# A gated feed-forward block: 19 of 22 gate-and-up pairs as seven quadrant products

## The chip, the cores and the metric

The kernel runs on one core of one Trainium2 chip, in one launch. The metric is device time in microseconds (us). Engines: TensorE (PE) multiplies, with PSUM banks as its output; VectorE (DVE), ScalarE (ACT) and GpSimd (POOL) do the elementwise work; SyncE (SP) and POOL issue DMAs. Each engine runs its own instructions strictly in program order and waits on semaphores for the others.

## The reference, cut to what matters

Two layers over 512 tokens of width 1024, each with a token mixer, a cross-attention and a gated feed-forward block. The change lies in the last one:

```python
D_MODEL = 1024; SEQ = 512; DEPTH = 2
D_FF = 2816                      # worked out: 22 blocks of 128 features

def swiglu_ffn(u, w_gate_up, w_down):
    g, up = jnp.split(u @ w_gate_up, 2, axis=-1)
    return (jax.nn.silu(g) * up) @ w_down

for i in range(DEPTH):
    ...                          # mixer, cross-attention
    u = rms_norm(h, ffn_pre_g[i])
    y = swiglu_ffn(u, w_gate_up[i], w_down[i])
    h = h + rms_norm(y, ffn_post_g[i])
```

## The kernel before

All matrices are float32. PE takes them in a rounded form (float32r), so each operand is split into a high part, a rounded copy, and a low part, the rest. A product is then three matmuls: high by high, low by high, high by low. A split is one ACT copy and one subtraction, mostly on DVE, for weights (L238, L239, in `issue`) as for activations (L201, L202, in `split`).

The normed activations u of a layer stand transposed in `uh` and `ul`: 128 partitions, 8 blocks k of 128 input features, 512 tokens. `norm_block` makes them a block of 128 tokens at a time: a square sum on ACT (L266), mean and power on POOL (L273, L278), scaling on DVE (L299), PE transposes (L285), and the split of these (L289, L290).

A weight tile is 128x1024, 512 KB: 8 blocks k for 128 output features. `plan` is the list of all weight tiles in the order of use. `fetch` loads them on SP's queue (L222) into one of two staging buffers `raw0` and `raw1`, and `issue` splits them into a ring of three pairs `wh`, `wl`. `used` gives a ring buffer back. A later tile is loaded as soon as the subtraction has left its staging buffer.

`ffn_up` makes gate and up for 22 pairs of feature blocks: 44 weight tiles, gate and up by turns, in `feats`. The output is features by tokens, 128x512, one PSUM bank. For each tile there are 8 blocks k times three matmuls of 512 columns (L313, L314, L315). The first three tiles run in two halves of 256 tokens, since the second half of u isn't normed yet; the norm's last transposes come between these matmuls. The silu of gate is an ACT instruction (L1065), its product with up a DVE one (L1069), and the split of that product (L201, L202) follows at once, into the tiles `r0` to `r21`.

`close` is the down product: 11 chunks of weights, each with two blocks k of 128 features, four token blocks and 24 matmuls of 512 columns (L365 to L367). Its first weights are loaded and split while `ffn_up` still runs. The gates of its spare weight buffers are in `ffn_spares`.

Instructions are written in this order by generators that `drive` runs. A scheduler then sets each engine's order from its own estimates; PE's order stays as written only where `pin` says so, which is not the case in the steady part of `ffn_up`.

Of the kernel before, what the change touches and what calls it, by code (L numbers as in the profile page):

```python
# [7 lines left out]
F32 = mybir.dt.float32  # L8
F32R = mybir.dt.float32r
# [9 lines left out]
NB = S // P  # L19
DK = D // P  # L20
FT = 22
NMEM = 256
EPS = 1e-6
NEG = -1e30
# [17 lines left out]
class Null:  # L42
# [3 lines left out]
    def __call__(self, *a, **k):  # L46
        return Null()


class Trunk:  # L50
    def __init__(self, tc, t, stack):
        self.tc = tc
        self.t = t
        pool = stack.enter_context(tc.tile_pool(name="sb", bufs=1))
        psum = stack.enter_context(
            tc.tile_pool(name="ps", bufs=1, space=bass.MemoryType.PSUM)
        )

        def sb(name, shape, dt=F32):
            return pool.tile(shape, dt, name=name)  # L60

        self.h = [sb(f"h{b}", [P, D]) for b in range(NB)]
# [12 lines left out]
        self.rc = sb("rc", [P, S])  # L75
        self.rs = sb("rs", [P, S])
        self.small = sb("small", [P, 160])
        self.qz = [sb(f"qz{i}", [P, 2, S], F32R) for i in range(2)]
        self.half = sb("mhalf", [P, 1])
        self.lam = sb("lam", [P, 1])  # L80
        self.gsub = sb("gsub", [P, 1])
        self.bank = [psum.tile([P, S], F32, name=f"bank{i}") for i in range(8)]

    def run(self):
        self.plan = []
        self.nc, self.planning = Null(), True
        self.emit()
        self.nc, self.planning = self.tc.nc, False
        self.emit()

    def reset(self):
# [10 lines left out]
        self.sbanks = self.bank[4:6]  # L102


    def pick(self, what, items):
# [102 lines left out]

    def plain(self, i):

        return None if self.planning else self.pool.tile([P, D], F32, name=f"m{i}", tag=f"r{i}")

    def restore(self, i):
        if not self.planning:
# [2 lines left out]
    def staging(self, i):  # L217
        return self.extra[i - 2] if i in (2, 3, 4) else self.raw[i % 2]

    def fetch(self, upto):  # L220
        while not self.planning and self.loaded < min(upto, len(self.plan)):
            self.nc.sync.dma_start(self.staging(self.loaded), self.plan[self.loaded][0])  # L222
            self.loaded += 1

    def issue(self):
        while not self.planning and self.issued < len(self.plan):
# [11 lines left out]
            self.nc.scalar.activation(hi, raw, AF.Copy)  # L238
            (self.nc.gpsimd if eng else self.nc.vector).tensor_tensor(  # L239
                lo, raw, hi.bitcast(F32), ALU.subtract  # L240
            )
# [105 lines left out]
            evac(bank)  # L347


    def close(self, w, ktiles, act, ready, gpost, gnext, spares, between=None):  # L350

        nc = self.nc
        yg = self.f[0:4]
# [93 lines left out]
    def setup(self):  # L447
# [3 lines left out]

        self.extra = [self.plain(i) for i in (4, 5, 6)]
        nc.vector.memset(self.half, -0.5)
        for z in self.qz:
            nc.gpsimd.memset(z[64:128, 0].bitcast(F32), 0.0)
            nc.gpsimd.memset(z[0:64, 1].bitcast(F32), 0.0)
        x(0)
        g = None
        for w in self.FIRST:
# [360 lines left out]
    def mixer(self, kind, wqk, wv, memory):  # L820
        hd = 64 if kind == 0 else 128
        if kind == 1:
            self.ones = self.mask[:, 0:P]
            self.nc.vector.memset(self.ones, 1.0 / P)

# [224 lines left out]
    XORDER = "k2 q1 k3 q2 q3"  # L1050


    def a_slot(self, k):
        return self.R[16 + k] if k < 6 else self.R[2 + k] if k < 14 else self.R[k - 14]

    def ffn_up(self, w):
        nc = self.nc
        keep = {}

        def evac(i):  # L1060
# [12 lines left out]
            return fn  # L1073

        yield from self.feats([(w[i], evac(i)) for i in range(2 * FT)], 3)

    def emit(self):
        self.reset()
# [3 lines left out]
            return self.R[k][:, 0], self.R[k][:, 1]  # L1082

        def a_act(k):
            return self.a_slot(k)[:, 0], self.a_slot(k)[:, 1]

        def o_ready(k):
            return ("o", k) in self.mark
# [13 lines left out]
        def has(*key):  # L1102
# [15 lines left out]
        ]  # L1118
        ffn_spares = [
            (None, None),  # L1120
            ((8, 9), has("n1", 3)),
            ((16, 17), has("n1", 0)),
            ((18, 19), has("n1", 1)),
            ((20, 21), has("n1", 2)),
        ]

        self.setup()
# [2 lines left out]
        for i in range(2):  # L1130
# [38 lines left out]
            self.drive(dense, self.x_attention(), self.RATE[2])  # L1169
            for k in range(11):  # L1170
                self.mark.pop(("n1", k), None)
            if i == 0:
# [4 lines left out]
            self.drive(  # L1177
                chain(
                    self.ffn_up(t["gate_up"][i]),
                    self.close(  # L1180
                        t["down"][i], FT, a_act, None, get("ffn_post_g"),
                        get("mix_pre_g") if i == 0 else None, ffn_spares,
                    ),
                )
            )
# [26 lines left out]

def alternate(a, b):
    return np.stack([a, b], 1).reshape((2 * a.shape[0],) + a.shape[1:])


def constants():
# [14 lines left out]
def layout(i):  # L1232
# [8 lines left out]
    for n in "ab":  # L1241
# [11 lines left out]
    r["gate_up"] = np.stack(  # L1253
        [alternate(feature_tiles(w[:, :ff]), feature_tiles(w[:, ff:])) for w in i["w_gate_up"]]
    )
# [25 lines left out]
```

## Time and profile before

| what | value |
|---|---|
| median of 3 runs | 1648.62 us (1646.05 to 1649.39) |
| profiled execution | 1650.47 us, its span 1648.7 us |
| PE busy | 1607.1 us, 97% |
| DVE, ACT, POOL busy | 54%, 42%, 17% |
| HBM read | 148.51 MB |

The profile is one execution. In its rows "L313" is line 313 of the kernel; buffer numbers are left out of names; "idle before <-" is the time in which the engine stood still before this group and what released it. In the timeline a row is start, length, engine, line, operation, output and inputs, shape and count. Matmuls overlap, so the time of one is the distance between starts. The gate-and-up stages are at about 473 to 715 us and 1281 to 1522 us.

### The profile page before, as it was taken

The numbers are of one execution on the slowest core, as the hardware profiler recorded it, in microseconds if no ns is written. First come the engines' busy times: TensorE is split into PE (matmuls) and PEld (weight loads), VectorE is DVE, ScalarE is ACT, GpSimd is POOL, SyncE is SP. The second block draws the span as 40 slices with busy tenths as digits, with TensorE's granted clock in tenths as the row PEclk, the third lists the DMA queues.
The fourth block names the chain that finished last, engine by engine and source line by source line (L and its number), as shares of the span: only waits on it lengthen the run. The fifth ranks groups of instructions, "written<-read, shape, count | busy, mean of one in ns | idle before, by whom it ended". The sixth has DMA issues, their size and how long they took to land.

```text
span 1648.7 us, 22174 instructions
## 1 busy us (share of the span) xinstructions
PE 1607.1 (97%) x8696; PEld 1384.9 (84%) x8696; DVE 896.1 (54%) x1414; ACT 696.9 (42%) x1211; POOL 276.3 (17%) x268
## 2 busy tenths in 40 slices
PE   6999989999999999999999999989999999999998
PEld 6899878899888888888798888778987988888886
DVE  7778886745553333322367888856555433333233
ACT  4566665544443232222336565634444322323121
POOL 4634420200010000000044654320001000000000
PEclk9999999999999999999999999999999999999999
DMA  5533423333312323222424434333331232232322
GB/s 217 150 89 103 112 76 107 116 115 100 118 64 94 102 90 103 95 98 99 131 87 134 123 98 115 100 105 104 115 115 65 77 103 92 100 101 92 103 89 89
DMA packets 54856, 172.49 MB, mean 105 GB/s; under 512 B 7520, under 2 KB 7776, under 8 KB 54752
## 3 DMA queue, kind: packets, MB, share of 16 engines
q1 hardware_dynamic: 54752, 171.08, 32.6%
q8 instruction: 68, 1.11, 0.3%
q14 instruction: 36, 0.29, 0.1%
HBM read 148.51 MB, written 2.10 MB: 91 GB/s over the span
## 4 chain that ended last, share of the span: by engine, by line
PE 81%; DVE 8%; DMA 3%; POOL 3%; issue 3%; ACT 2%; SPq 0%; POOLq 0%; DVEq 0%; ACTq 0%
PE bank L314 14%; PE bank L313 14%; PE bank L315 14%; PE bank L365 7%; PE bank L367 7%; PE bank L366 7%; PE bank L285 4%; PE bank L725 2%; PE bank L651 1%; PE bank L652 1%; DVE wl L239 1%; PE bank L634 1%; PE bank L635 1%; PE bank L920 1%; PE bank L633 1%
## 5 line engine op out<-in xcount | busy, mean ns | idle before, releaser
L238 ACT ACTIVATE wh<-raw 128x1024 fp32r<-128x1024 f32 x231 | 244.6, 1059 | 551.7 <-PE bank L314 224.2
L239 DVE TENSOR_TENSOR wl<-raw,wh 128x1024 fp32r<-128x1024 f32 x204 | 257.1, 1260 | 354.5 <-ACT wh L238 353.7
L313 PE MATMUL bank<-uh,wh 128*128 128x512 f32 (+1 forms) x1184 | 443.2, 375 | 0.4 <-ACT uh L289 0.4
L314 PE MATMUL bank<-ul,wh 128*128 128x512 f32 (+1 forms) x1184 | 442.7, 374 | 0.0
L315 PE MATMUL bank<-uh,wl 128*128 128x512 f32 (+1 forms) x1184 | 442.6, 374 | 0.0
L313 PEld LDWEIGHTS bank<-uh,wh 128*128 128x128 f32 x1184 | 223.7, 189 | 39.5 <-ACT uh L289 0.8
L315 PEld LDWEIGHTS bank<-uh,wl 128*128 128x128 f32 x1184 | 223.8, 189 | 38.2 <-issue 0.5
L314 PEld LDWEIGHTS bank<-ul,wh 128*128 128x128 f32 x1184 | 223.8, 189 | 38.0 <-DVE ul L290 0.3
L273 POOL TENSOR_SCALAR small<-small 128x1 f32<-128x1 f32 x76 | 24.2, 318 | 1105.3 <-ACT junk L266 1105.1
L365 PE MATMUL bank<-wh,r 128*128 128x512 f32 x400 | 157.9, 396 | 1.2 <-DVE f L761 0.8
L366 PE MATMUL bank<-wl,r 128*128 128x512 f32 x400 | 156.8, 392 | 0.0
L367 PE MATMUL bank<-wh,r 128*128 128x512 f32 x400 | 155.0, 392 | 0.0
L285 PE MATMUL bank<-ident,f 128*128 128x128 f32 x576 | 95.8, 282 | 22.8 <-DVE f L299 17.4
L1069 DVE TENSOR_TENSOR f<-f,bank 128x512 f32<-128x512 f32 x44 | 30.3, 688 | 142.6 <-PE bank L315 141.1
L285 PEld LDWEIGHTS bank<-ident,f 128*128 128x128 f32 x576 | 71.3, 144 | 33.5 <-DVE f L299 20.1
L365 PEld LDWEIGHTS bank<-wh,r 128*128 128x128 f32 x400 | 75.6, 189 | 18.5 <-DVE f L761 1.6
L366 PEld LDWEIGHTS bank<-wl,r 128*128 128x128 f32 x400 | 75.7, 189 | 15.0 <-issue 0.2
L367 PEld LDWEIGHTS bank<-wh,r 128*128 128x128 f32 x400 | 75.3, 189 | 15.4
L365 PE MATMUL bank<-r,r 128*128 128x512 f32 x208 | 83.7, 403 | 0.0
L366 PE MATMUL bank<-r,r 128*128 128x512 f32 x208 | 81.9, 394 | 0.4 <-DVE r L239 0.4
L367 PE MATMUL bank<-r,r 128*128 128x512 f32 x208 | 80.1, 395 | 0.0
L289 ACT ACTIVATE r<-bank 128x512 fp32r<-128x512 f32 x104 | 60.7, 592 | 38.2 <-PE bank L285 33.1
(173 smaller groups left out, 2764.7 us busy)
## 6 DMA issues: line engine op xcount, KB each, us to landing
raw<-in_gate_up SPq DMA_DIRECT2D x88, 512.0 KB, 3.2
raw<-in_down SPq DMA_DIRECT2D x44, 512.0 KB, 3.2
r<-r SPq DMA_DIRECT2D x120, 128.0 KB, 2.3
raw<-in_x_wk SPq DMA_DIRECT2D x16, 512.0 KB, 3.3
raw<-in_x_wv SPq DMA_DIRECT2D x16, 512.0 KB, 3.3
raw<-in_x_wq SPq DMA_DIRECT2D x16, 512.0 KB, 3.3
raw<-in_x_wo SPq DMA_DIRECT2D x16, 512.0 KB, 3.3
raw<-in_b_qk SPq DMA_DIRECT2D x16, 512.0 KB, 3.4
```

The source lines that it names most:

```text
L238: self.nc.scalar.activation(hi, raw, AF.Copy)
L239: (self.nc.gpsimd if eng else self.nc.vector).tensor_tensor(lo, raw, hi.bitcast(F32), ALU.subtract)
L285: nc.tensor.transpose(tb[:, k * P : (k + 1) * P], u[:, k * P : (k + 1) * P], self.ident)
L289: nc.scalar.activation(hi, tv, AF.Copy)
L313: nc.tensor.matmul(out, wh[:, k], xh(k)[:, cols], start=k == 0, stop=False)
L314: nc.tensor.matmul(out, wh[:, k], xl(k)[:, cols], start=False, stop=False)
L315: nc.tensor.matmul(out, wl[:, k], xh(k)[:, cols], start=False, stop=k == DK - 1)
L365: nc.tensor.matmul(out, ah[:, ts], hi[:, kk], start=k == 0, stop=False)
L366: nc.tensor.matmul(out, ah[:, ts], lo[:, kk], start=False, stop=False)
L367: nc.tensor.matmul(out, al[:, ts], hi[:, kk], start=False, stop=k == ktiles - 1)
L725: nc.tensor.matmul(out, w, m, start=kb == 0 and s == 0, stop=kb == 3 and s == 1)
L1069: nc.vector.tensor_mul(a, a, bank)
```

## The change

The first three pairs of a layer (NP) stay as they were. For the other 19 (NS) a pair is taken as one 2x2 block matrix: its rows are gate and up features (128 each), its columns the two halves of the input features (four blocks k each); u is split likewise by input halves and token halves of 256. One level of Strassen's method in Winograd's form then needs seven products of quadrants instead of eight. Each has 4 blocks k and three matmuls of 256 columns (L1206 to L1208 in `s_product`).

The seven weight operands are four quadrants and three sums. They are held as seven columns of 512 in a page (`fold`); two pages take turns, and one of them is the memory that held `raw0`, `raw1`, the mask and the junk tile, the other that of the `qz` tiles. `s_load` fills a page: SP loads 512 KB into columns 3 and 4 (L1155), 512 KB into 2 and 6 (L1156) and 256 KB into 0 (L1160), and a DMA from POOL's queue adds another 512 KB to columns 3 and 4 (L1161). `s_sums` makes columns 1 and 5 by two DVE additions (L1168, L1169). `s_parts` splits the columns, two at a time into `wh`, `wl` and the last into `r13` (L229 on ACT, L230 on DVE).

The activations' operands are quadrants of `uh`, `ul` and four sums. `fold` makes these, once a layer, during the three plain pairs: it joins high and low of the quadrants by four POOL additions (L1124), makes the sums on DVE and splits them. In `s_pair` products are collected in PSUM where the method lets two of them share a bank; ACT copies the first product (L1226), DVE makes the other sums (L1228, L1235, L1241, L1243, L1251) and the product with silu (L1109).

The silu product stays unsplit in the tiles `m`; `close` calls `a_split` two chunks ahead, which splits one tile of 128x1024 there. The first loads for `close` begin when the last pair starts to release its buffers. The lines of unchanged code move: L222 is now L253, L239 L270, L273 and L278 are L304 and L309.

On DVE, in the steady part of gate-and-up, before, four rows a pair (`wl` is the low part of a weight tile, `f` holds silu and product, `r` the split product):

```order
L239 TENSOR_TENSOR wl0_94<-raw1_90,wh0_91 128x1024 [waits DMAHW2_49,PE_49,Activation_49]
L1069 TENSOR_TENSOR f1_100<-f1_100,bank0_120 128x512 [waits PE_49,Activation_49]
L239 TENSOR_TENSOR wl1_95<-raw0_89,wh1_92 128x1024 [waits DMAHW3_49,Activation_49]
L202 TENSOR_TENSOR r20_87<-f1_100,r20_87 128x512 [waits Activation_49]
```

and what stands there for one pair after (fold12 is being split and multiplied, fold13 loaded and summed; DMAHW is a load of SP's queue, DMASW the adding DMA):

```order
L230 TENSOR_TENSOR wl1_93<-fold12_5520,wh1_90 128x1024 [waits DMAHW3_49,Activation_49]
L1235 TENSOR_TENSOR f5_102<-f6_103,bank5_121 128x256 [waits PE_49]
L230 TENSOR_TENSOR wl2_94<-fold12_5520,wh2_91 128x1024 [waits Activation_49]
L1241 TENSOR_TENSOR f3_100<-bank7_123,f5_102 128x256 [waits DVE_49,PE_49]
L1228 TENSOR_TENSOR f6_103<-bank1_117,f4_101 128x256 [waits PE_49,Activation_49]
L1243 TENSOR_TENSOR f5_102<-bank5_121,f6_103 128x256 [waits DVE_49,PE_49]
L1168 TENSOR_TENSOR fold13_5628<-fold13_5628 128x512 [waits DMAHW5_49,DMASW5_49]
L230 TENSOR_TENSOR wl0_92<-fold12_5520,wh0_89 128x1024 [waits Activation_49]
L1251 TENSOR_TENSOR f3_100<-bank7_123,f6_103 128x256 [waits PE_49]
L1169 TENSOR_TENSOR fold13_5628<-fold13_5628 128x512 [waits DVE_49]
L230 TENSOR_TENSOR r13_80<-fold12_5520,r13_80 128x512 [waits Activation_49]
L1109 TENSOR_TENSOR m7_4143<-f1_98,f3_100 128x512 [waits DVE_49]
```

Four rows a pair became twelve, and L1168 of the next fold, which waits for its adding DMA, stands ahead of the last two subtractions of this one (into wl0 and r13).

The DMAs that fill fold13 on SP, after:

```order
L1155 DMA fold13_5628<-in_gate_up_s 128x1024 [waits DMAHW0_49,DMAHW7_49,DMASW3_49,DVE_49]
L1156 DMA fold13_5628<-in_gate_up_s 128x2x512
L1160 DMA fold13_5628<-in_gate_up_s 128x512 [waits DMAHW6_49]
```

and on POOL's queue:

```order
L1161 DMA fold13_5628<-in_gate_up_s 128x1024 [waits DMAHW4_49,DMAHW0_49,DMAHW7_49,DMASW3_49,DVE_49]
```

The first waits for DVE's last use of fold11, which lay in the same page; the adding DMA waits for the first to land.

On POOL, from the norm before the first gate-and-up stage, before (means and powers of the norms of token blocks):

```order
L273 TENSOR_SCALAR small_114<-small_114 128x1 [waits Activation_49]
L278 TENSOR_TENSOR small_114<-small_114,mhalf_117 128x1 [waits Pool_49]
L273 TENSOR_SCALAR small_114<-small_114 128x1 [waits Activation_49]
L278 TENSOR_TENSOR small_114<-small_114,mhalf_117 128x1 [waits Pool_49]
L273 TENSOR_SCALAR small_114<-small_114 128x1 [waits Activation_49]
L278 TENSOR_TENSOR small_114<-small_114,mhalf_117 128x1 [waits Pool_49]
```

and after:

```order
L1124 TENSOR_TENSOR m3_4139<-uh_65,ul_66 128x1024 [waits DVE_49,PE_49]
L304 TENSOR_SCALAR small_110<-small_110 128x1 [waits Activation_49]
L1124 TENSOR_TENSOR m6_4142<-uh_65,ul_66 128x1024 [waits DVE_49,PE_49]
L309 TENSOR_TENSOR small_110<-small_110,mhalf_113 128x1 [waits Pool_49]
L304 TENSOR_SCALAR small_110<-small_110 128x1 [waits Activation_49]
L309 TENSOR_TENSOR small_110<-small_110,mhalf_113 128x1 [waits Pool_49]
```

Two of the four joins came in ahead of the mean and of the power of block 2; the other two follow the last power.

The diff, cut to what computes, loads and orders:

```diff
-        self.raw = [sb(f"raw{i}", [P, D]) for i in range(2)]
-        self.junk = sb("junk", [P, D], BF16)
-        self.mask = sb("mask", [P, 896])
-        self.qz = [sb(f"qz{i}", [P, 2, S], F32R) for i in range(2)]
+        self.pages = [
+            pool.tile([P, 7 * S], dt, name=f"page{i}", tag=f"page{i}") for i, dt in ((0, F32), (1, F32R))
+        ]
...
+    def page0(self):
+        x = self.pages[0]
+        self.raw = [x[:, :D], x[:, D : 2 * D]]
+        self.mask = x[:, 2 * D : 2 * D + 896]
+        self.junk = x[:, 2 * D + 896 : 2 * D + 896 + S].bitcast(BF16)
...
                 for b in range(NB):
                     yield from mm(b, c, wt, banks[b])
+                    if b == 1:
+                        ahead(c + 2)
...
+    def a_split(self, c):
+        if c >= len(self.PLAIN):
+            return
+        src = self.hidden[c].rearrange("p (a b) -> p a b", a=2)
+        self.split(src, *self.a_pair(c))
+        self.restore(self.PLAIN[c])
+        self.mark["a", c] = self.clock
+    def a_out(self, f, s, up):
+        a = self.hidden[f // 2][:, (f % 2) * S : (f % 2) * S + S]
+        self.nc.vector.tensor_mul(a, s, up)
...
+    SUMS = ((14, 15), (18, 21), (8, 9), (16, 17))
+    def fold(self, step):
+        nc = self.nc
+        v = lambda t: t.rearrange("p (k t) -> p k t", k=4)
+        r = {n: self.hidden[i] for n, i in (("11", 3), ("21", 4), ("22", 5), ("12", 6), ("s", 7))}
+        def join(n):
+            i, j = int(n[0]) - 1, int(n[1]) - 1
+            ks, ts = slice(4 * j, 4 * j + 4), slice(256 * i, 256 * i + 256)
+            nc.gpsimd.tensor_tensor(
+                v(r[n]), self.uh[:, ks, ts].bitcast(F32), self.ul[:, ks, ts].bitcast(F32), ALU.add
+            )
+        def part(src, which):
+            hi, lo = [self.R[i].rearrange("p a b -> p (a b)") for i in self.SUMS[which]]
+            self.split(src, hi, lo)
+        if step == 0:
+            for n in ("21", "22", "11", "12"):
+                join(n)
+            nc.vector.tensor_sub(r["s"], r["21"], r["22"])
+            part(r["s"], 1)
+        elif step == 1:
+            nc.vector.tensor_sub(r["22"], r["11"], r["s"])
+            part(r["22"], 2)
+        elif step == 2:
+            nc.vector.tensor_sub(r["11"], r["11"], r["21"])
+            part(r["11"], 0)
+        else:
+            nc.vector.tensor_sub(r["12"], r["12"], r["22"])
+            part(r["12"], 3)
+    def s_load(self, s):
+        if s >= NS:
+            return
+        nc = self.nc
+        x = self.page((s + 1) % 2, f"fold{s}")
+        self.fw[s] = x
+        src = self.fsrc[s]
+        nc.sync.dma_start(x[:, 3 * S : 5 * S], src[:, 2 * S :])
+        nc.sync.dma_start(
+            x[:, 2 * S :].rearrange("p (a b) -> p a b", b=S)[:, 0::4],
+            src[:, : 2 * S].rearrange("p (a b) -> p a b", b=S),
+        )
+        nc.sync.dma_start(x[:, :S], src[:, 3 * S :])
+        nc.gpsimd.dma_start(x[:, 3 * S : 5 * S], src[:, S : 3 * S], accum_op=ALU.add)
+    def s_sums(self, s):
+        if s >= NS:
+            return
+        x = self.fw[s]
+        c = [x[:, i * S : (i + 1) * S] for i in range(7)]
+        self.nc.vector.tensor_add(c[1], c[4], c[6])
+        self.nc.vector.tensor_add(c[5], c[1], c[2])
+    def s_parts(self, s, g):
+        if s >= NS:
+            return
+        x = self.fw[s]
+        if g < 3:
+            b = self.fbuf[g]
+            hi, lo, x = self.wh[b], self.wl[b], x[:, g * D : (g + 1) * D]
+        else:
+            hi, lo, x = self.R[13][:, 0], self.R[13][:, 1], x[:, 6 * S :]
+        self.split(x, hi, lo)
...
+    def s_product(self, bank, n, act, first=True):
+        nc = self.nc
+        wh, wl = self.s_weight(n)
+        xh, xl = self.s_act(act)
+        out = bank[:, :256]
+        skip = {"skip_group_check": True}
+        for k in range(4):
+            nc.tensor.matmul(out, wh[:, k], xh[:, k], start=first and k == 0, stop=False, **skip)
+            nc.tensor.matmul(out, wh[:, k], xl[:, k], start=False, stop=False, **skip)
+            nc.tensor.matmul(out, wl[:, k], xh[:, k], start=False, stop= k == 3, **skip)
+            yield 0.36
+    def s_pair(self, s):
+        nc = self.nc
+        X, Y, Z, V = [
+            self.bank[i][:, :256] for i in ((0, 1, 2, 6) if (NS - 1 - s) % 2 == 0 else (3, 4, 5, 7))
+        ]
+        sil = self.pick("sil", self.f[0:2])
+        cc = self.pick("cc", self.f[2:4])
+        pw = self.pick("pw", self.f[4:6])
+        p1, w = pw[:, :256], pw[:, 256:]
+        v = self.pick("v", [self.f[6][:, :256], self.f[6][:, 256:]])
+        t1, t2 = slice(0, 256), slice(256, 512)
+        last = s == NS - 1
+        if s == 0:
+            self.s_sums(1)
+        yield from self.s_product(X, 0, "11")
+        nc.scalar.activation(p1, X, AF.Copy)
+        yield from self.s_product(Y, 1, 2)
+        nc.vector.tensor_sub(v, Y, p1)
+        self.s_parts(s + 1, 0)
+        if last:
+            self.release(0)
+        yield from self.s_product(X, 2, "12", False)
+        nc.scalar.activation(sil[:, t1], X, AF.Silu)
+        yield from self.s_product(Z, 3, 0)
+        nc.vector.tensor_sub(w, v, Z)
+        self.s_parts(s + 1, 1)
+        if last:
+            self.release(1)
+            self.a_split(0)
+        yield from self.s_product(V, 4, 1)
+        nc.vector.tensor_add(cc[:, t2], V, w)
+        yield from self.s_product(Z, 5, "22", False)
+        nc.vector.tensor_sub(w, Z, v)
+        nc.scalar.activation(sil[:, t2], w, AF.Silu)
+        self.s_parts(s + 1, 2)
+        self.s_sums(s + 2)
+        if last:
+            self.release(2)
+            self.a_split(1)
+        yield from self.s_product(V, 6, 3, False)
+        nc.vector.tensor_add(cc[:, t1], V, v)
+        self.a_out(NP + s, sil, cc)
+        self.s_parts(s + 1, 3)
+        self.s_load(s + 3)
...
+        def after(i):
+            if i < 4:
+                self.fold(i)
+            if i == 2:
+                self.s_load(1)
+                self.s_sums(0)
+            if i >= 3:
+                self.s_parts(0, i - 3)
+            if i == 5:
+                self.s_parts(0, 3)
+                self.s_load(2)
...
                 else:
-                    a = keep[f]
-                    nc.vector.tensor_mul(a, a, bank)
-                    t = self.a_slot(f)
-                    self.split(a, t[:, 0], t[:, 1])
+                    self.a_out(f, keep[f], bank)
+                after(i)
...
-        yield from self.feats([(w[i], evac(i)) for i in range(2 * FT)], 3)
+        self.s_load(0)
+        yield from self.feats([(w[i], evac(i)) for i in range(2 * NP)], 3)
...
+        for s in range(NS):
+            if s == NS - 1:
+                self.page(0, "page0")
+                self.page0()
+            yield from self.s_pair(s)
...
+def folded_tiles(g, u):
+    n = len(g)
+    g, u = [x.reshape(n, P, 2, 4 * P) for x in (g, u)]
+    return np.stack([g[:, :, 1], u[:, :, 1], u[:, :, 0], g[:, :, 0]], 2).reshape(n, P, 4 * 4 * P)
```

More of the change, by code (lines that the diff above doesn't have):

```diff
@@ L21 @@
 FT = 22
+NP = 3
+NS = FT - NP
 NMEM = 256
@@ L89, in run, with page, page1 @@
         self.emit()
+    def page(self, i, name, dt=F32):
+        if not self.planning:
+            self.pages[i] = self.pool.tile([P, 7 * S], dt, name=name, tag=f"page{i}")
+        return self.pages[i]
+    def page0(self):
[3 more added lines that the diff above has]
+        self.junk = x[:, 2 * D + 896 : 2 * D + 896 + S].bitcast(BF16)
+    def page1(self):
+        x = self.pages[1]
+        self.qz = [x[:, i * D : (i + 1) * D].rearrange("p (a b) -> p a b", a=2) for i in range(2)]
+        for z in self.qz:
+            self.nc.gpsimd.memset(z[64:128, 0].bitcast(F32), 0.0)
+            self.nc.gpsimd.memset(z[0:64, 1].bitcast(F32), 0.0)
     def reset(self):
@@ L102, in reset @@
         self.sbanks = self.bank[4:6]
+        self.hold = self.hold_at.get(0)
     def pick(self, what, items):
@@ L218, in staging, with limit @@
         return self.extra[i - 2] if i in (2, 3, 4) else self.raw[i % 2]
+    def limit(self):
+        return len(self.plan) if self.hold is None else self.hold
     def fetch(self, upto):
-        while not self.planning and self.loaded < min(upto, len(self.plan)):
+        while not self.planning and self.loaded < min(upto, self.limit()):
             self.nc.sync.dma_start(self.staging(self.loaded), self.plan[self.loaded][0])
@@ L225, in issue @@
     def issue(self):
-        while not self.planning and self.issued < len(self.plan):
+        while not self.planning and self.issued < self.limit():
             i = self.issued
@@ L347, in feats, with close @@
             evac(bank)
-    def close(self, w, ktiles, act, ready, gpost, gnext, spares, between=None):
+    def close(self, w, ktiles, act, ready, gpost, gnext, spares, between=None, ahead=None):
         nc = self.nc
@@ L453, in setup @@
         nc.vector.memset(self.half, -0.5)
-        for z in self.qz:
-            nc.gpsimd.memset(z[64:128, 0].bitcast(F32), 0.0)
-            nc.gpsimd.memset(z[0:64, 1].bitcast(F32), 0.0)
+        self.page0()
+        self.page1()
         x(0)
@@ L822, in mixer @@
         if kind == 1:
+            self.page(1, "qz", F32R)
+            self.page1()
             self.ones = self.mask[:, 0:P]
@@ L1057, in ffn_up, with release @@
+    def release(self, g):
+        if self.planning:
+            return
+        if g == 0:
+            self.hold = self.hold_at.get(self.layer + 1)
+            self.busy |= set(self.fbuf)
+        self.busy.discard(self.fbuf[g])
+        self.issue()
+    def ffn_up(self, layer, w, ws):
         nc = self.nc
         keep = {}
+        self.fw = {}
+        self.fsrc = ws
+        self.layer = layer
+        if self.planning:
+            self.turn[layer] = self.nring
+        n = self.turn[layer] + 2 * NP
+        self.fbuf = [(n + g) % 3 for g in range(3)]
+        self.hidden = [self.plain(i) for i in self.PLAIN]
+        def after(i):
[9 more added lines that the diff above has]
+                self.s_load(2)
@@ L1084, in a_act @@
         def a_act(k):
-            return self.a_slot(k)[:, 0], self.a_slot(k)[:, 1]
+            return [x[:, k % 2] for x in self.a_pair(k // 2)]
         def o_ready(k):
@@ L1120, in emit @@
             (None, None),
[L1121 to L1124, printed above, removed]
+            ((7, 10), has("a", 8)),
+            ((11, 12), has("a", 10)),
+            ((19, 20), has("n1", 0)),
+            ((8, 9), has("n1", 1)),
         ]
```

46 lines of the change are left out of this document (37 added, 9 removed).

## The prediction

> **What bounds the kernel now.** I read the page's busy shares and its chain first, then both layers' gate-and-up stages by stretches of time, then single matmuls, then the groups of that stage by form.
>
> ```profile
> PE 1607.1 (97%) x8696; PEld 1384.9 (84%) x8696; DVE 896.1 (54%) x1414; ACT 696.9 (42%) x1211; POOL 276.3 (17%) x268
> PE 81%; DVE 8%; DMA 3%; POOL 3%; issue 3%; ACT 2%; SPq 0%; POOLq 0%; DVEq 0%; ACTq 0%
> 500.00:720.00 220.00, 220.00 (x973) 182.15 (x972) 74.81 (x80) 63.22 (x81) 0.00 (x0) 1.00 0.29 96
> 1300.00:1520.00 220.00, 220.00 (x972) 182.24 (x971) 76.04 (x81) 64.09 (x82) 0.00 (x0) 1.00 0.30 98
> ```
>
> The last two rows are 220 us each, all but some 5 of them gate-and-up, in layer 0 and in layer 1 (busy PE, weight loads, DVE, ACT, POOL, then granted clock, DMA share, GB/s). TensorE (PE) never stops, at clock 1.00, while VectorE (DVE) works a third of the time, GpSimd (POOL) not at all, and DMA 0.30. So here, and only while the others stay hidden, a matmul saved is time saved. What a matmul costs is read from start to start, since each row's own length overlaps its neighbours:
>
> ```profile
> 599.62 0.39 PE L314 MATMUL bank<-ul,wh 128*128 128x512 f32 x1
> ...
> 605.97 0.39 PE L315 MATMUL bank<-uh,wl 128*128 128x512 f32 x1
> ```
>
> ```profile
> 1284.83 0.28 PE L315 MATMUL bank<-uh,wl 128*128 128x256 f32 x1
> ...
> 1286.99 0.28 PE L315 MATMUL bank<-uh,wl 128*128 128x256 f32 x1
> ```
>
> 28 steps in 6.35 us: 0.227 us for 512 columns. 18 steps in 2.16 us: 0.120 us for 256.
>
> **The matmuls.** A pair was 48 of 512 columns, 48 x 0.2268 = 10.88 us; it becomes 7 products x 4 x 3 = 84 of 256, 84 x 0.120 = 10.08. That is 0.80 saved a pair, 38 pairs, 30.4 us in all: the most that the change can gain, since a halved matmul costs 53% of a whole one, not 50%. The Trainium skill ("TensorE: Matmul & The Clock Gate", section "Back-to-back issue gap") gives N/2.4 + 2.5 ns, by which a pair would save 1.19 us and all 45; the trace has 120 ns where that says 109, and the trace decides.
>
> **What the other engines get.** Rows of the stage by form (count, busy us, mean ns), two of half width from elsewhere, and a POOL subtraction:
>
> ```profile
> L239 DVE TENSOR_TENSOR wl<-raw,wh 128x1024 fp32r<-128x1024 f32 x40 | 49.0, 1225 | 75.7 <-ACT wh L238 75.7
> L202 DVE TENSOR_TENSOR r<-f,r 128x512 fp32r<-128x512 f32 x20 | 13.7, 685 | 0.0
> L238 ACT ACTIVATE wh<-raw 128x1024 fp32r<-128x1024 f32 x41 | 43.5, 1061 | 159.8 <-PE bank L314 76.8 <-issue 73.7 <-PE bank L367 5.2
> L201 ACT ACTIVATE r<-f 128x512 fp32r<-128x512 f32 x20 | 12.7, 633 | 0.0
> L202 DVE TENSOR_TENSOR r<-bank,r 128x256 fp32r<-128x256 f32 x32 | 13.5, 421 | 21.9 <-ACT r L201 21.7
> L201 ACT ACTIVATE r<-bank 128x256 fp32r<-128x256 f32 x32 | 12.3, 384 | 34.7 <-PE bank L1007 31.3 <-DVE r L202 3.4
> L239 POOL TENSOR_TENSOR wl<-raw,wh 128x1024 fp32r<-128x1024 f32 x27 | 66.6, 2471 | 49.1 <-ACT wh L238 45.9 <-ACT r L289 3.1
> ```
>
> DVE for a pair, now: three subtractions of 128x1024 (3 x 1.225), four of 128x512 (the fourth weight group, both weight sums, the silu product; 4 x 0.685) and five evictions of 128x256 (5 x 0.421): 8.52 us of 10.08, against 3.8 of 10.88. ACT: 3 x 1.061 + 0.633 + 3 x 0.384 = 4.97, hidden. Down: it now splits the silu products, one 128x1024 (1.06 on ACT, 1.23 on DVE) for each of its chunks of two features blocks, beside 24 matmuls x 0.227 = 5.4 us: DVE has that and the chunk's own weight, 2 x 1.23 = 2.45, ACT 2.1. Hidden, and if it weren't, it would cost at most 11 x 2.3 x 2 = 50 us. The sums of the activations after the first pairs' products are covered by the three plain pairs, 3 x 10.9 us.
>
> **The chain that is new.** A pair's seven weight operands take 1.75 MB from HBM rather than 1 MB, into one of two pages. By the order of DVE and SP shown with the change, the load of page k+1 waits for the last subtraction (r13) of weights k-1, since they lie in the same page. The adding DMA waits until that load has landed. L1168 of k+1 waits for the adding DMA, and DVE, in order, keeps behind it: subtraction wl0 (1.225), L1251 (0.421), L1169 (0.685), subtraction r13 (0.685). With L1168 itself (0.685) that is 3.70 us until r13 lets the next load go. So a ring closes once a pair, and its length is
>
> load + adding DMA (X) + hops + 3.70.
>
> ```profile
> raw<-in_gate_up SPq DMA_DIRECT2D x88, 512.0 KB, 3.2
> r<-ul SPq DMA_DIRECT2D x2, 512.0 KB, 5.0
> 0.00:25.00 25.00, 12.87 (x75) 11.80 (x76) 15.08 (x29) 11.86 (x18) 11.16 (x18) 1.00 0.91 330
> ```
>
> The load is 512 KB, 3.2 us. Four hops between queues at about 0.1 us (1278.85 + 0.19 to 1279.13 in the POOL rows below is 0.09) are 0.4. Without X that is 7.3, so the ring stays under PE's 10.08 only if X is below 2.8. X itself is in no row: nothing before adds in a DMA. Low end: 3.2, a plain 512 KB load; there is no reason for it to be quicker than that, though on a queue of its own it could be, so 2.0 or less isn't excluded by anything but that row. High end: 5.0, the two 512 KB copies within SBUF, which like the adding DMA read SBUF, and beyond, because two more loads (768 KB) leave SP right behind the first: at the 330 GB/s of the third row they hold the engines 2.4 us. I take 4.6, nearer the upper row, since the transfer reads two operands and shares the engines with those loads.
>
> DVE's order isn't the same in all 17 links of a layer: from L1168 to r13 I add by the same durations 5.23, 2.21, 5.35, 1.37, 4.39, 0, 2.06, 1.79, 4.12, 4.12, then 3.70 seven times (0 where r13 stands ahead of L1168). Each link takes the larger of 10.08 and 3.6 + X + that. Seventeen links and the two pairs outside them, against 19 x 10.88 = 206.7 us a layer, for two layers:
>
> - X = 2.0: 193.1, -27 us; X = 3.2: 201.3, -11;
> - X = 3.7: 207.3, +1 (here the gain is gone);
> - X = 4.6: 218.6, **+24**; X = 5.0: 224.5, +36; X = 5.8: 237.2, +61.
>
> The Trainium skill ("DMA: Bandwidth & Descriptors", section "Anatomy of one DMA — SWDGE (gpsimd) path") puts a GpSimd DMA at 2.0 us + bytes/436e3, which is 3.2 us here and the -11 line. Its page "Collectives: The Full Stack" (section "The bandwidth ceiling: the fold count and why AG ≠ RS ≠ AR") says that an add, needing two source reads, runs at half the rate of a copy; an estimate from both is 4.4 us and +18. No run here shows either.
>
> **The joins on POOL.** Four POOL additions of 128x1024 (2.47 us by the L239 row) start the stage, two of them ahead of the norm of token block 2, in POOL's queue:
>
> ```profile
> 1277.44 1.28 DVE L290 TENSOR_TENSOR ul<-bank,uh 128x512 fp32r<-128x512 f32 x2
> 1278.85 0.19 POOL L273 TENSOR_SCALAR small<-small 128x1 f32<-128x1 f32 x1 [2.78 <-ACT junk L266]
> 1279.13 0.55 POOL L278 TENSOR_TENSOR small<-small,mhalf 128x1 f32<-128x1 f32 x1
> 1279.70 1.41 DVE L299 SCALAR_TENSOR_TENSOR f<-h,small,g 128x512 f32<-128x512 f32 x2 [0.98 <-POOL small L278]
> 1280.50 0.28 PE L313 MATMUL bank<-uh,wh 128*128 128x256 f32 x1
> 1280.85 0.60 PE L285 MATMUL bank<-ident,f 128*128 128x128 f32 x4
> ...
> 1287.47 0.60 PE L285 MATMUL bank<-ident,f 128*128 128x128 f32 x4
> ```
>
> The first join can start when half of ul is there, 1278.1, and ends at 1280.6; then the mean (0.2), the second join to 1283.3, then the power to 1283.8 instead of 1279.68. L299 follows at 1283.9 instead of 1279.70, and the transposes of block 2, which stood three matmuls into the new stage, start 4.2 later less the 0.4 in which they had not been waited for: PE stalls 3.8 us. Block 3's transposes start 6.6 us after block 2's and have that shift already. Both layers have this order: +7.6. Between 0 (POOL done sooner) and 10 (each join 2.5, nothing absorbed). The page "SBUF — State Buffer" of the Trainium skill (section "Who interferes with whom") has a GpSimd instruction that reads SBUF held up by a DVE one with two SBUF inputs, which could lengthen the joins.
>
> **Sum.** 1650.47 (the profiled execution, span 1648.7 and 1.8 around it) + 23.7 + 7.6 = 1681.8; it lay 1.85 above the median of the runs, so 1680.
>
> **Rivals.**
> 1. The adding DMA hides (the other side): X under 2.8, or DVE's r13 in fact earlier than I count, and PE bounds as before: -30.4, or -23 with the POOL stall: 1618 to 1626. For it: DMA at 0.30, POOL idle, 16 engines free. Against it: both rows of 512 KB are above 2.8. It decides at X = 3.3 with the stall, 3.7 without; up to there it is faster.
> 2. X is that of a plain load, 3.2: -11 + 7.6, 1645, on the edge of what can be told from no change. For it: the row of that size. Against it: the second operand and the loads beside it. This is also what the fit on the Trainium skill's page "DMA: Bandwidth & Descriptors" would give.
> 3. DVE is late by itself. Its 8.52 us leave 1.56 for waits on PE in each pair, and it now empties PSUM five times a pair where each of seven products waits for it. 2 us of waits more than that would make pairs of 12: +1.2 x 38 = +46, 1695. Against it: two sets of four banks.
> 4. X of 5.2 to 5.8, the two samples' upper end and the loads beside it: +42 to +61, with the stall 1698 to 1717.
>
> **Chances.** About 0.2% (3 us) is what can be told from no change. The forecast (X from 3.8 to 5.2, its own range 1655 to 1698) 0.44; rival 1 0.23; rival 2 0.13, of which 0.05 faster, 0.07 same, 0.01 slower; rivals 3 and 4 0.20. Faster 0.28, same 0.07, slower 0.65. The range takes in part of rival 1 and most of 4: 1628 to 1715.
>
> **What would show it.** In the profile after, 256-column steps of 0.120; PE idle before L1206 to L1208, released by DVE's r13 or wl0; DVE idle before L1168, released by DMA; pairs 11 to 13 us apart. L1161 to landing near 4.6 us. POOL L1124 about 2.5 us x4 and a gap of some 4 us in PE at the first 256-column matmuls of the stage. I am wrong if DVE never waits at L1168, or L1161 lands in under 3 us, or PE is at 10.1 a pair.

## The result, and the profile after

The changed kernel takes 1748.79 us (median, 1746.4 to 1750.19), the one before 1649.01 beside it: ratio 1.0606, interval 1.0588 to 1.0625. That is 100 us slower, on the forecast's side, and 34 us beyond the range's upper end. Of the page after, these are the busy shares and the DMAs that fill the folds (KB each, median us from issue to landing, that is until all data has arrived; the first row takes L1155 and L1156 together, L1155 alone takes 3.9):

```profile
PE 1623.9 (93%) x10064; PEld 1460.3 (84%) x10064; DVE 1091.5 (62%) x1750; ACT 778.8 (45%) x1349; POOL 331.1 (19%) x318
...
fold<-in_gate_up_s SPq DMA_DIRECT2D x76, 512.0 KB, 4.6
...
fold<-in_gate_up_s POOLq DMA_DIRECT2D x38, 512.0 KB, 6.3
```

By stretches of time, these are the two layers' seven-product stages, with the columns as in the prediction:

```profile
513.40:766.00 252.60, 215.00 (x1609) 207.68 (x1608) 150.91 (x230) 93.98 (x138) 16.88 (x21) 0.94 0.52 133
1366.50:1626.00 259.50, 221.97 (x1610) 215.69 (x1609) 151.98 (x231) 94.38 (x139) 14.79 (x17) 0.90 0.51 129
```

PE, which had no idle time here before, is idle for 37.6 and 37.5 us, and its granted clock is 0.94 and 0.90 where it was 1.00. Who waits is in the list of waits over the whole kernel (us in total, times, longest):

```profile
DVE fold L1168 <- DMA fold<-in_gate_up_s: 148.3, 37, 6.6
...
PEld bank L1208 <- DVE wl L230: 64.6, 40, 3.4
...
PE bank L1208 <- DVE wl L230: 55.9, 39, 3.2
```

DVE waits at the first weight sum for the adding DMA, and PE for a subtraction behind it in DVE's queue. One turn of the ring in the timeline of DVE, SP and POOL:

```profile
648.36 0.68 DVE L230 TENSOR_TENSOR r<-fold,r 128x512 fp32r<-128x512 f32 x1
...
649.07 0.33 SPq L1155 DMA_DIRECT2D fold<-in_gate_up_s  x1
...
653.88 0.87 POOL L1161 DMA_DIRECT2D fold<-in_gate_up_s  x1 [13.50 <-issue]
...
660.16 0.69 DVE L1168 TENSOR_TENSOR fold<-fold 128x512 f32<-128x512 f32 x1 [5.17 <-DMA fold<-in_gate_up_s]
660.77 1.22 DVE L230 TENSOR_TENSOR wl<-fold,wh 128x1024 fp32r<-128x1024 f32 x1
661.91 0.42 DVE L1251 TENSOR_TENSOR f<-bank,f 128x256 f32<-128x256 f32 x1
662.24 0.68 DVE L1169 TENSOR_TENSOR fold<-fold 128x512 f32<-128x512 f32 x1
662.84 0.68 DVE L230 TENSOR_TENSOR r<-fold,r 128x512 fp32r<-128x512 f32 x1
```

r13 ends at 649.04 and L1155 is issued at 649.07. The adding DMA starts 4.81 later and L1168 6.28 after that; the next r13 ends at 663.52. The turn is 14.48 us: 3.36 on DVE (its rows overlap by a tenth each, against my 3.70) and 11.1 in DMAs, where I had 8.2.

Starts of PE's matmuls give where the time went (us; "product" means L1206, "down" the last L365 or L396):

| | before, layer 0 | after, layer 0 | before, layer 1 | after, layer 1 |
|---|---|---|---|---|
| three plain pairs with the norm's end | 36.3 | 41.1 | 35.4 | 41.1 |
| the other 19 pairs | 206.7 | 256.7 | 206.7 | 263.2 |
| from the last pair to the last down matmul | 124.5 | 113.4 | 119.0 | 111.2 |

Before, the first two are parted by calculation, 19 x 10.88; in layer 0 gate-and-up runs from 469.90 to 712.96 us there. The 19 pairs cost 106.5 more, the plain pairs 10.5, and down is 18.9 shorter. But PE's order isn't fixed there, and in each layer 36 of down's matmuls now run among those of the last pair: that pair takes 18.3 us, which is its own 84 x 0.120 and 36 x 0.227 without a wait. These 16.3 us are only moved. Without them the 19 pairs cost 90.2 more, and down itself is 2.6 shorter.

### The profile page after: what moved, and what is told of

Read it like the earlier page. It is cut to its first block, busy times and chain, and to the rows that moved or that the text cites. A ratio compares the mean times of both kernels' runs of the same rounds, so it can differ in the third digit from the quotient of the medians.

```text
span 1748.3 us, 25719 instructions
## 1 busy us (share of the span) xinstructions
PE 1623.9 (93%) x10064; PEld 1460.3 (84%) x10064; DVE 1091.5 (62%) x1750; ACT 778.8 (45%) x1349; POOL 331.1 (19%) x318
## 5 line engine op out<-in xcount | busy, mean ns | idle before, releaser
L270 DVE TENSOR_TENSOR wl<-page,wh 128x1024 fp32r<-128x1024 f32 x128 | 164.2, 1284 | 168.9 <-ACT wh L269 168.1
L269 ACT ACTIVATE wh<-page 128x1024 fp32r<-128x1024 f32 x155 | 163.6, 1057 | 218.0 <-PE bank L398 87.6
L229 ACT ACTIVATE wh<-fold 128x1024 fp32r<-128x1024 f32 x114 | 119.8, 1056 | 200.0 <-PE bank L1207 88.1
L344 PE MATMUL bank<-uh,wh 128*128 128x512 f32 (+1 forms) x576 | 208.0, 362 | 0.3 <-ACT uh L320 0.3
L345 PE MATMUL bank<-ul,wh 128*128 128x512 f32 (+1 forms) x576 | 207.4, 360 | 0.0
L346 PE MATMUL bank<-uh,wl 128*128 128x512 f32 (+1 forms) x576 | 207.0, 360 | 0.0
L1208 PE MATMUL bank<-r,wl 128*128 128x256 f32 x456 | 136.2, 300 | 37.9 <-DVE wl L230 37.9
L1206 PE MATMUL bank<-uh,wh 128*128 128x256 f32 x456 | 138.1, 303 | 18.5 <-ACT wh L229 11.5
L1208 PE MATMUL bank<-uh,wl 128*128 128x256 f32 x456 | 138.0, 305 | 18.0 <-DVE wl L230 17.9
L230 DVE TENSOR_TENSOR wl<-fold,wh 128x1024 fp32r<-128x1024 f32 x114 | 138.5, 1217 | 12.8 <-ACT wh L229 12.7
L304 POOL TENSOR_SCALAR small<-small 128x1 f32<-128x1 f32 x76 | 24.8, 326 | 641.3 <-ACT page L297 640.8
L1206 PE MATMUL bank<-r,wh 128*128 128x256 f32 x456 | 136.5, 300 | 0.7 <-ACT wh L229 0.7
L1207 PE MATMUL bank<-ul,wh 128*128 128x256 f32 x456 | 136.8, 300 | 0.0
L1207 PE MATMUL bank<-r,wh 128*128 128x256 f32 x456 | 135.7, 298 | 0.0
L396 PE MATMUL bank<-wh,r 128*128 128x512 f32 x336 | 130.8, 394 | 3.1 <-DVE f L802 2.2
L1208 PEld LDWEIGHTS bank<-r,wl 128*128 128x128 f32 x456 | 93.0, 204 | 41.7 <-DVE wl L230 41.6
L1161 POOL DMA_DIRECT2D fold<-in_gate_up_s x38 | 33.5, 881 | 491.5 <-DMA fold<-in_gate_up_s 121.4
L345 PEld LDWEIGHTS bank<-ul,wh 128*128 128x128 f32 x576 | 110.9, 193 | 14.4 <-issue 0.2
```

What stands on the lines that cost most here:

```text
L230: self.nc.vector.tensor_sub(lo, src, hi.bitcast(F32))
L270: (self.nc.gpsimd if eng else self.nc.vector).tensor_tensor(lo, raw, hi.bitcast(F32), ALU.subtract)
L344: nc.tensor.matmul(out, wh[:, k], xh(k)[:, cols], start=k == 0, stop=False)
L345: nc.tensor.matmul(out, wh[:, k], xl(k)[:, cols], start=False, stop=False)
L346: nc.tensor.matmul(out, wl[:, k], xh(k)[:, cols], start=False, stop=k == DK - 1)
L396: nc.tensor.matmul(out, ah[:, ts], hi[:, kk], start=k == 0, stop=False)
```

## The experiments

The theory was that the ring sets the pace, and the rivals that DVE is late by itself, that 1.75 MB a pair is too much, or that the place of the adding DMA doesn't matter. The plain pairs are the three unchanged ones ahead of the 19; X is the adding DMA's time, as in the prediction. First the ring was opened by leaving something out, then by order alone.

**Without the adding DMA** (e2):

```diff
-        nc.gpsimd.dma_start(x[:, 3 * S : 5 * S], src[:, S : 3 * S], accum_op=ALU.add)
```

> The adding DMA (L1161) is left out, so columns 3 and 4 hold one quadrant each instead of a sum; everything else, and every wait but those for that DMA, stays. Theory (the ring load, adding DMA, L1168, r13 sets the pace): the ring of the changed kernel's trace, 4.8 us load + 5.7 us adding DMA + 3.7 us on DVE = 14.2, loses 5.7 and is 8.9 with the second load's landing, under PE's 10.08 a pair. Then PE bounds: 1650 - 30 + 8.6 for POOL's joins, about 1628 us. Rival 1 (DVE with its twelve rows a pair is late by itself): pairs of about 12 us, 1690 or more. Rival 2 (the pace is that of the loads, 1.75 MB a pair): little change, above 1720.

1632.53 us, ratio 0.9913 (0.9893 to 0.9933). By stretches of time the two stages are:

```profile
514.00:714.00 200.00, 198.42 (x1623) 196.51 (x1622) 150.62 (x230) 94.56 (x140) 2.09 (x4) 1.00 0.37 123
1312.00:1511.00 199.00, 198.68 (x1626) 196.93 (x1625) 150.39 (x229) 94.32 (x140) 0.00 (x0) 1.00 0.37 124
```

With the same 150 us of DVE work PE is idle for 1.6 and 0.3 us only, at clock 1.00. All of the loss hangs on this DMA; DVE's rows and the other 1.25 MB fit.

**A plain DMA in its place** (e3):

```diff
-        ... src[:, S : 3 * S], accum_op=ALU.add)
+        ... src[:, S : 3 * S])
```

> The adding DMA becomes a plain one from the same queue: same bytes, place, waits and order, but it overwrites columns 3 and 4, so the sum is left out. Theory that the addition makes it long: issue to landing falls from 6.3 to about 4 us, each link that is bound by the ring loses about 2 us, 17 links in 2 layers: 1749 - 2 x 16 x 2 = about 1690 us. Rival (POOL's queue and the two loads beside it make it long, the addition nothing): 6.3 us again and 1749.

1683.93 us, ratio 1.0217 (1.0196 to 1.0237). These are the times from issue to landing of L1161 in layer 0, first in the changed kernel, then plain:

```profile
DMA to landing us min/median/max: 5.4/6.2/6.5
```

```profile
DMA to landing us min/median/max: 3.8/4.1/5.5
```

The addition makes 2.1 us of it, and that alone 65 us of the time. The prediction's sum with 3.9 load, 0.75 to POOL's start and 4.05 to L1168 gives 205.8 us for the 17 links of a layer; from the first L1168 to the last the trace has 203.7 and 203.4.

**Every pair with the first one's operands** (e5):

```diff
-        if s >= NS:
+        if s >= 1:
             return
```

(in `s_load`, `s_sums` and `s_parts`)

> Every pair uses the operands of the first one: loads, weight sums and weight splits of the other 18 pairs a layer are left out, and with them the ring and most of DVE's and ACT's work. PE does all 84 matmuls a pair. If a 256-column matmul costs 0.120 us here as in the norm's halves, 1650 - 30 + 8.6 = 1628 us. Below that would mean that I priced the matmuls too high, above 1640 that PE's gain is not there at all.

1633.95 us, ratio 0.9917 (0.9901 to 0.9932), as without the adding DMA. PE is never idle in this stage of layer 0; the last three rows are down's matmuls in its last pair:

```profile
516.00:711.00 195.00, 195.00 (x1610) 194.24 (x1609) 63.21 (x122) 32.33 (x67) 2.08 (x4) 1.00 0.02 7
```

```profile
L396 PE MATMUL bank<-wh,r 128*128 128x512 f32 x7 | 2.4, 391 | 0.0
L397 PE MATMUL bank<-wl,r 128*128 128x512 f32 x6 | 2.3, 390 | 0.0
L398 PE MATMUL bank<-wh,r 128*128 128x512 f32 x6 | 2.3, 390 | 0.0
```

Starts of PE's matmuls put the first 18 pairs at 10.08 us each; the last takes 14.4, since these 19 matmuls of down (4.3 us) run in it. So the price of 0.120 held, and the 38 pairs save the 30 us that the prediction had. The time is still 6 us above my 1628: the plain pairs cost 12 us rather than 8.6, and in the profiled executions 4.7 lie in the stages ahead of the gate-and-up ones, where nothing was changed.

**Joins after the norm** (e4):

```diff
+            for n in ("11", "12"):
+                nc.vector.tensor_copy(r[n][:, 0:1], self.ul[:, 7, S - 1 : S].bitcast(F32))
             for n in ("21", "22", "11", "12"):
                 join(n)
```

> Two one-column DVE copies ahead of the joins of quadrants 11 and 12 make these two wait for the norm's last block; POOL then does all means and powers first. Theory: PE's stalls of 4.32 and 4.30 us before the transposes of block 2 go, the joins stay hidden beside the plain pairs: 1749 - 8.6 = 1740 us. Rival: the joins come late for the activation sums, which then are late for the first product: no change or slower, 1749 to 1755.

1748.0 us, ratio 1.0612 (1.0596 to 1.0628): no change. The stall was there as forecast; this PE row of the changed kernel is block 2's transposes in layer 0:

```profile
476.89 0.66 PE L316 MATMUL bank<-ident,f 128*128 128x128 f32 x4 [4.04 <-DVE f L330]
```

It is gone in e4, and the plain pairs take 37.8 and 36.7 us instead of 41.1 and 41.1, 7.7 less. But the first of the 19 pairs now takes 12.5 and 14.4 us instead of 10.1, as its adding DMAs come no sooner (in layer 0 the first starts at 508.0 us for 507.3), and the 19 pairs take 261.0 and 261.6, together 2.7 more. Another 4.1 lie in the stages ahead of gate-and-up, where nothing was changed; what makes them I haven't traced. And DVE rows beside the joins that now run in one go are nearly three times as long:

```profile
488.39 3.42 DVE L1137 TENSOR_TENSOR m<-m,m 128x1024 f32<-128x1024 f32 x1 [3.48 <-POOL m L1124]
491.73 3.44 DVE L270 TENSOR_TENSOR wl<-page,wh 128x1024 fp32r<-128x1024 f32 x1
...
495.69 1.21 DVE L1140 TENSOR_TENSOR m<-m,m 128x1024 f32<-128x1024 f32 x1
```

**Two lasting tiles** (e1):

```diff
-        x = self.page((s + 1) % 2, f"fold{s}")
+        x = self.page((s + 1) % 2, f"fold{s}") if s < 2 else self.fw[s - 2]
```

> A layer's folds use two tiles for good, rather than a new tile of the same memory for each fold, so that a load waits for the readers of its own columns only: L1155 for the subtraction into wl0 and no longer for r13. The same work and sums. Theory of the ring: the scheduler now puts L1168 of the next fold ahead of that subtraction too, so the ring only loses what lies between the two, 10.5 of loads and 3.0 of DVE rows (L1168, L1243, L1169, wl0) instead of 3.7: 0.7 us x 16 links x 2 = -22, about 1727 us. Rival (the release of the whole tile is what costs): the ring opens, 1632.

1764.4 us, ratio 1.0708 (1.0689 to 1.0727): a miss of both. L1155 did go sooner after its subtraction (wl0), but the scheduler put L1168, L1243 and L1169 ahead of that one. The ring held: 4.4 to the adding DMA's start, 6.4 to L1168 and 3.0 on DVE are 13.8, and the mean distance of the sums is 13.9 us against 13.7 in the changed kernel. My expectation took the steady links' 3.70 for all; by my own count the 17 links average 3.33, and less with the rows' overlap, so there was nothing left to gain. Of the 12.4 us between the two profiled executions the 19 pairs account for 6.3, the plain pairs for 1.8 and the stages ahead of gate-and-up for 3.9; why the latter are longer isn't shown.

**Sums behind the last split, PE and DVE in written order** (e7):

```diff
         self.s_parts(s + 1, 2)
-        self.s_sums(s + 2)
...
         self.s_load(s + 3)
+        self.s_sums(s + 2)
...
+        fixed = self.tc.manual_schedule(engines={PE, DVE})   # around pairs 0 to 17
```

> Only the place of the two weight sums: written behind the last split (r13), with PE's and DVE's order kept as written in the 18 pairs. New tile for each fold, adding DMA and joins as in the changed kernel. Theory: L1168, waiting for its adding DMA, no longer holds back the subtraction that lets the next load go; a ring then takes two pairs, 2 p = 10.5 + about 9.7 of DVE, so p is 10.1 to 10.4 and PE is nearly the bound: 1632 to 1650 us. Rival (the adding DMA costs because transfers and PE or DVE disturb each other, wherever it stands): above 1700.

1636.89 us, ratio 0.9936 (0.9923 to 0.9948), with every load and sum in place. Rows of DVE and POOL, and then both stages by stretches of time:

```profile
639.74 0.68 DVE L1168 TENSOR_TENSOR fold<-fold 128x512 f32<-128x512 f32 x1
...
644.63 0.86 POOL L1161 DMA_DIRECT2D fold<-in_gate_up_s  x1 [9.43 <-DMA fold<-in_gate_up_s]
...
649.28 0.69 DVE L230 TENSOR_TENSOR r<-fold,r 128x512 fp32r<-128x512 f32 x1
...
650.74 0.69 DVE L1168 TENSOR_TENSOR fold<-fold 128x512 f32<-128x512 f32 x1 [0.78 <-DMA fold<-in_gate_up_s]
```

```profile
515.00:713.00 198.00, 197.80 (x1616) 196.41 (x1615) 157.58 (x231) 98.20 (x140) 16.91 (x21) 1.00 0.65 169
1314.00:1514.00 200.00, 197.75 (x1611) 195.77 (x1610) 157.99 (x231) 97.48 (x140) 14.82 (x17) 1.00 0.65 168
```

The adding DMA is as long as ever, 6.1 us to landing, and the queue the same. But r13 now stands ahead of the L1168 that waits for it, so the next load goes out meanwhile, and the wait is 0.8 us instead of 5.2. Most pairs take 10.13 us. The kernel is 6% faster than the changed one and 0.6% faster than the one before, little, but with an interval clear of 1. The edit moves the sums and also fixes PE's order; what the latter does by itself isn't parted here.

**Order and lasting tiles** (e9), the last two edits together:

> The order of sums behind r13 and the two lasting tiles together; the joins on POOL as in the changed kernel. The load may start after wl0, some 2 us sooner: nearly a period and 2 us, 11.9, for 10.5 of loads. PE bounds, as in the kernel without the adding DMA: 1632 us, now with the whole computation. Rival (DVE's twelve rows don't fit a pair in order): 1650 or more.

1637.53 us, ratio 0.9932 (0.9918 to 0.9945): nothing more than by order alone, and 5 us above my 1632.

**These and the late joins** (e8):

> As the one with order and tiles, and the joins wait for the norm's last block. With PE as the bound the two stalls of 4.3 us before the transposes of block 2 should show now: 1632 - 8.6 = 1624 us. Rival: POOL's late joins hold up DVE's subtractions (3.42 instead of 1.21 us beside them in the run with late joins alone) and the first seven-product pair starts no sooner: 1632.

1636.43 us, ratio 0.9931 (0.9919 to 0.9943). The plain pairs are 3.9 and 4.4 us shorter than in e9, and the products 4.7 and 4.5 longer: in layer 0 the second fold's sum waits for its adding DMA, and PE for a DVE row behind it:

```profile
519.18 0.69 DVE L1170 TENSOR_TENSOR fold<-fold 128x512 f32<-128x512 f32 x1 [5.46 <-DMA fold<-in_gate_up_s]
...
521.25 0.39 PE L1208 MATMUL bank<-r,wh 128*128 128x256 f32 x1 [1.79 <-DVE m L1109]
```

(L1170 and L1208 are L1168 and L1206 there.) So the stall that I priced at 7.6 us covers the first folds' chain, which otherwise is waited for; layer 1, whose first pair takes 15.7 us, I haven't traced.

**The two other loads left out** (e10), in the kernel with lasting tiles:

```diff
+        if s < 2:
             nc.sync.dma_start(... columns 2 and 6 ...)
             nc.sync.dma_start(x[:, :S], src[:, 3 * S :])
```

> The kernel with two lasting tiles, and the two loads behind the first (columns 2 and 6, and 0) left out after the first two folds, so the adding DMA and its load are alone on the engines; the other columns keep old data. Theory that these loads share the engines with them: load to adding DMA falls from 4.4 to about 3.6, adding DMA to L1168 from 6.4 to about 5, a ring of 11.6 instead of 13.9, about 1680 us. Rival (the two times are the transfers' own): 4.4 and 6.4 stay, 1764.

1744.12 us, one run, between my two figures. From the load's issue to the adding DMA's start it is 4.35 us (4.37 with the loads), from there to L1168 6.1 (6.4), both as medians. L1155, then L1161 (L1162 there), take this from issue to landing:

```profile
DMA to landing us min/median/max: 3.5/3.7/5.3
```

```profile
DMA to landing us min/median/max: 5.2/6.1/6.9
```

So the loads beside them are not why the two are long. They cost something, though: the sums are 13.3 us apart instead of 13.9, which over 34 links makes about 19 of the 20 us below e1's 1764, and most of it is in the mean time from the adding DMA's start to L1168, 5.9 instead of 6.6.

**The addition on DVE** (e11), the order of e7 without the adding DMA:

```diff
-        nc.gpsimd.dma_start(... accum_op=ALU.add)
+        nc.sync.dma_start(... columns 1 and 5 ..., src[:, S : 3 * S] ...)
...
+        self.nc.vector.tensor_add(v, v, y)   # columns 3, 4 += 1, 5
```

> As the kernel with the sums behind r13, but without the adding DMA: SP loads the addend into columns 1 and 5, which are free until the sums, and DVE adds it there (128x1024, 1.22 us). The whole computation. DVE then has 9.7 us a pair of PE's 10.3, in order. Theory (PE bounds, waits on PE fit): 1632 to 1645 us, about the time of the one with the adding DMA. Rival 3 of the prediction (DVE's waits on PE don't fit into what is left): pairs of 11 us or more, 1660 or more.

1646.57 us, ratio 0.9993 (0.9982 to 1.0003). Sixteen of a layer's pairs take 10.50 us and a little more, of which DVE works 9.1, and once a pair PE waits for an eviction that DVE does behind a subtraction:

```profile
530.00:690.00 160.00, 157.60 (x1280) 154.54 (x1278) 139.26 (x199) 73.51 (x107) 0.00 (x0) 1.00 0.52 178
```

```profile
606.32 0.39 PE L1212 MATMUL bank<-uh,wh 128*128 128x256 f32 x1 [0.35 <-DVE f L1241]
```

(L1212 and L1241 are L1206 and L1235 there.) So with 1.2 us more DVE work a pair than in e7 rival 3 begins to be true, though by far less than its 11 us a pair: the time lies between my two figures.

## Why the prediction was right and where it was wrong

- Side and mechanism were right: the ring of load, adding DMA, L1168 and r13, its 17 links, and PE behind them. e2 and e7 open it in two ways, and both bring PE back to clock 1.00 and next to no gaps.
- The step that failed is the size of the ring, and most of it is "X itself is in no row ... I take 4.6": X is 6.2 to landing. I had the second operand's cost as part of a guess between a load and a copy within SBUF, and held the upper row for near the end; e3 shows 4.1 for the plain DMA of that queue and 2.1 for the addition.
- Step "the load is 512 KB, 3.2 us. Four hops ... 0.4": the load takes 3.9 to landing, and POOL starts the adding DMA 0.75 later, where I had taken a hop's price from two POOL instructions in a row. Together with X that is 10.85 instead of 8.2. Why the load takes 3.9 here and not 3.2 isn't shown; in e10, with no load right behind it, it still takes 3.7.
- Put into the prediction's own sum, 10.85 gives 241.0 us for the 17 links of a layer; from the first L1168 to the last the trace has 231.5 and 236.0. So the form of the sum was right, and 2 to 4% long; that DVE's rows overlap (3.36 for 3.70 in a steady link) goes that way. For all 19 pairs the sum then gives +109 for both layers, where the trace has +90.2 without down's matmuls; that it has +106.5 with them is chance. Of the 67 us by which the sum's +31 fell short of the +98 of the table, the pairs make all: +90.2 for +23.7. X was too small, and the range's upper end (X = 5.8) too. Each us of X counts some 30 times, so a range for X from two rows was too narrow.
- The transfer "shares the engines with those loads": a small reason, 0.6 us a turn in e10, and not what made X long.
- The joins: the stall is 4.04 and 4.02 us of idle PE for 3.8 forecast, and the plain pairs cost 10.5 for +7.6. But the term can't be taken away by itself: without the stall the kernel isn't faster (e4, e8), since the first folds' chain is waited for instead.
- The matmuls: right. A pair without waits takes 10.08 us (e5), so the gain of 30 that all rivals started from is there. Rival 1's time of 1618 to 1626 would still have been 1633, as e2 has it: its pairs save 26.5 us and its plain pairs cost 12.
- Down: I had its splits hidden, and they are: it is 2.6 us shorter in all, with the 16.3 that moved into the last pairs counted to it. That PE would take these up there I hadn't seen.

The Trainium skill's fit ("DMA: Bandwidth & Descriptors", section "Anatomy of one DMA — SWDGE (gpsimd) path") gives 3.2 us for the plain DMA; the trace of e3 has 4.1. With the halved rate that the Trainium skill has ("Collectives: The Full Stack", section "The bandwidth ceiling: the fold count and why AG ≠ RS ≠ AR"), the estimate was 4.4 for the adding one; the trace has 6.2. That an add is dearer than a copy the runs bear out.

## What to carry to other kernels

DMA queues that are far from full can still set the pace: here an engine that works in order waited for a transfer, and behind the waiting instruction stood the very one that lets the next transfer go. Look for such a ring, add up its parts once around, and give the part that no row shows a range wide enough for the number of turns. And look at which instructions a stretch of time holds before comparing it with a sum. The remedy here was order, not a faster transfer: put the waiting instruction behind the one that releases.

## What the runs showed of the hardware

- After some waits PE runs slower for a while. In the changed kernel, around a wait of 3.2 us:

```profile
658.48 0.28 PE L1206 MATMUL bank<-r,wh 128*128 128x256 f32 x1
658.60 0.28 PE L1207 MATMUL bank<-r,wh 128*128 128x256 f32 x1
662.04 0.58 PE L1208 MATMUL bank<-r,wl 128*128 128x256 f32 x1 [3.17 <-DVE wl L230]
662.43 0.42 PE L1206 MATMUL bank<-r,wh 128*128 128x256 f32 x1
662.64 0.41 PE L1207 MATMUL bank<-r,wh 128*128 128x256 f32 x1
662.86 0.41 PE L1208 MATMUL bank<-r,wl 128*128 128x256 f32 x1
```

  The steps are 0.12 us before it and 0.21 after, for some 3 us, in which the granted clock is 0.50. Not every wait does this: after those that end at 598.25 and 622.47 us (2.4 and 1.6 us long) the steps are 0.12 again at once but for the first. What decides I haven't tested. What this adds to the time I can't part from the waits: the ring doesn't run through most of these matmuls.
- A DVE instruction with two operands in SBUF took 3.42 us instead of 1.21 while POOL added from SBUF (e4). The Trainium skill ("SBUF — State Buffer", section "Who interferes with whom") says that these two contend; the rows agree.
- A 512 KB adding DMA takes 6.2 us to landing (changed kernel), a plain one of the same queue 4.1 (e3), the first load of a fold on SP's queue 3.7 to 3.9.
